# Hybrid state-space block on one core: the head products of two units issued together, their decays and operands a job sooner

## The chip, the cores and the metric

The kernel runs on one core of a Trainium2 chip. The metric is the device time of one execution in microseconds, from the first to the last instruction of that core with what lies around them; less is better. Before the change three runs gave 1990.82, 1993.07 and 1993.24 us (median 1993.07 us).

## The reference, cut to what matters

One layer of a hybrid backbone: a normalised token stream goes through one input projection and is split between a state-space mixer (Mamba-2 style, 32 heads of 64 channels in 4 groups, state 128, chunks of 128 tokens, forward and backward) and a linear recurrent mixer; both are gated, merged, projected, and followed by a gated feed-forward. There are 256 latent and 256 context tokens, model width 2048, all in float32. The change concerns the state-space mixer alone:

```python
CB = jnp.einsum('bcign,bcjgn->bcijg', Cc, Bc)
y_diag = jnp.einsum('bcijg,bcijge,bcjgep->bcigep', CB, Lmat, xdt)
y_off = jnp.einsum('bcign,bcige,bcgepn->bcigep', Cc, jnp.exp(a_cum), entering)
return (y_diag + y_off).reshape(b_, L, G, E, P), final
```

`Lmat` holds the decays between two tokens of a chunk, `exp(a_cum)` those from the start of a chunk. For a latent chunk and a head the output is the sum of three products: the diagonal part (forward and backward decays in one matrix `G`), and the entering states of the two directions times `C` with its decays (`CE`).

## The kernel before, in words

**Projections.** TensorE works through a list of jobs. A job is one 128-column slice of a weight matrix against all 16 tiles of the contraction. `load` brings half a job (a piece, 128x1024 floats, `raw`, line 157) by SP's queue; `parts` splits it into a high part `wh` on ScalarE (line 173) and a low part `wl` on VectorE (line 174). The rings of `raw`, `wh` and `wl` hold four pieces each: the cast of a piece waits until TensorE is done with the piece four before it, and the load of a piece waits until VectorE has made the `wl` four before it. A "both" job (latent and context tokens, lines 188 to 190) and a "lat" job (latent alone, lines 192 to 194) multiply three times per tile of the contraction, a "packed" job (lines 206 and 209) twice. After a job its `evac` empties PSUM, and up to two `rawa` rows of a modulation matrix are multiplied and summed on VectorE (lines 473, loaded at 464); each `rawa` pair stands behind the low parts made so far.

**State-space groups.** For each of four groups of 8 heads there are six "both"/"lat" jobs (four slices of x, one of B, one of C). When the last is done, the group's own work is put into later gaps between jobs, its turns: turn 0 is right behind that job, turn n behind the n-th job after it. Group g's turn 6 is thus group g+1's turn 0; behind the last group come gate jobs ("lat") and then z jobs ("packed"). A turn's parts are issued one behind another on all engines; TensorE's order is the written one, while the order on ScalarE, VectorE and SP is made by a scheduler.

**A group's parts.** `context_tokens`, `context_states` and `carried_states` build transposes, states and the triangular products `U` and `L`. Then there are four units: unit 0 and 1 are chunk 0 and 1 of the first four heads, unit 2 and 3 those of the last four. Each unit has three parts:

- `fetch` (line 802): a DMA copies the unit's cumulated decays to all partitions, tile `AC`, 2 buffers. A third unit's fetch so waits for the first one's products.
- `operands`: ScalarE and VectorE make `E` (lines 811, 812), take two exponentials (line 107), multiply `AC` by `C` (line 817), make `G` from `U` and `L` (820, 821) and multiply it by `E` (line 823). `E` and `G` share 3 buffers.
- `products` (line 840): 24 short float32 matmuls, two heads side by side in the array's columns; VectorE adds the skip term (line 845), and after the second chunk the result goes to memory (line 848).

The turns stand in three tables: `LONG` for groups 0 and 1, `LAST_LONG` for group 2, `SHORT` for group 3. In each row of a table the first entry is for the activations, the second for the three context parts, and the third, fourth and fifth for products, fetch and operands of units 0 to 3.

Of the kernel before, what the change touches and what calls it, by code (L numbers as in the profile page):

```python
# [55 lines left out]
def hybrid_block(  # L56
# [639 lines left out]

    LONG = ((0,), (2, 3, 4), (5, 6, 7, 8), (3, 4, 5, 6), (4, 5, 6, 7))
    LAST_LONG = LONG[:2] + ((5, 6, 8, 10), (3, 4, 5, 7), (4, 5, 6, 8))  # L700
    SHORT = ((0,), (4, 5, 7), (9, 11, 13, 15), (6, 7, 9, 11), (7, 9, 11, 13))

    def xs_evac(g, t):
        def f(ps):
# [6 lines left out]
            if t == 3:  # L711
                when = LONG if g < NG - 2 else LAST_LONG if g < NG - 1 else SHORT
                for ns, fs in zip(when, ssd_group(g)):
# [437 lines left out]
```

## Time and profile before

| | |
|---|---|
| median of three runs | 1993.07 us (1990.82 to 1993.24) |
| the profiled execution: its time, its span | 1992.71 us, 1990.8 us |
| TensorE busy, share of the span | 1961.4 us, 99% |
| VectorE busy | 1425.0 us, 72% |
| ScalarE busy | 1101.9 us, 55% |
| HBM | 220 GB/s over the span |
| the state-space products (line 840) | from 548.1 to 817.1 us |

The busy share of TensorE says that it always had something in flight, not that it was at its peak: ends of matmuls are modelled, and a matmul that starts late or waits for its weights is counted as busy too. What a matmul costs the chain is read from the distance between two starts.

### The profile page before, as it was taken

What the parts mean: (1) busy time and instruction counts of PE and PEld (TensorE: products, weight loads), DVE (VectorE), ACT (ScalarE), POOL (GpSimd) and SP (SyncE); (2) the same over time, 40 slices, a digit from 0 to 9 for tenths busy, and PEclk for the clock granted to TensorE, in tenths of its full rate; (3) what the DMA queues carried; (4) which work ended last, traced back from release to release, by engine and by line L of the source; (5) the groups of instructions that cost most, each with busy time, mean ns of one, the idle gap of its engine ahead of it and who ended that gap; (6) DMA issues with size and microseconds to landing.
All of it is one profiled execution on the core that took longest, in us unless ns stands there. A gap on an engine that the chain in (4) does not pass through costs nothing.

```text
span 1990.8 us, 30569 instructions
## 1 busy us (share of the span) xinstructions
PE 1961.4 (99%) x11649; PEld 1671.6 (84%) x11649; DVE 1425.0 (72%) x2154; ACT 1101.9 (55%) x1663; POOL 3.9 (0%) x7
## 2 busy tenths in 40 slices
PE   7999999999999999999999999999999999999997
PEld 3678888898787798888888888888888888888887
DVE  5468899896767888988787788666666665555553
ACT  4346888784464666755655454544444444444442
POOL 0000000000000000000000000000000000000000
PEclk9999999999999999999999999999999999999999
DMA  9984444456454578899887775777776765566663
GB/s 371 353 289 149 136 155 159 139 187 198 141 163 138 180 223 259 300 322 352 282 288 258 258 266 184 229 235 237 237 233 228 241 219 190 179 188 184 188 192 118
DMA packets 143842, 440.32 MB, mean 221 GB/s; under 512 B 17488, under 2 KB 36176, under 8 KB 143568
## 3 DMA queue, kind: packets, MB, share of 16 engines
q1 hardware_dynamic: 143328, 437.91, 67.0%
q8 instruction: 91, 1.49, 0.3%
q10 hardware_dynamic: 368, 0.47, 0.1%
q14 instruction: 55, 0.45, 0.1%
HBM read 427.77 MB, written 10.55 MB: 220 GB/s over the span
## 4 chain that ended last, share of the span: by engine, by line
PE 58%; issue 38%; DMA 1%; DVE 1%; ACT 1%; POOL 0%; SPq 0%; POOLq 0%; DVEq 0%; ACTq 0%
PE ps L206 14%; PE ps L209 7%; PE ps L188 6%; PE ps L189 5%; PE ps L190 5%; PE ps L192 3%; PE ps L194 3%; PE ps L193 3%; PE ps L391 1%; PE pa L344 1%; PE ps L392 1%; PE ps L393 1%; PE py L840 1%; DMA raw<-in_dram 1%; PE lg L535 1%
## 5 line engine op out<-in xcount | busy, mean ns | idle before, releaser
L174 DVE TENSOR_TENSOR wl<-raw,wh 128x1024 fp32r<-128x1024 f32 (+1 forms) x566 | 677.4, 1199 | 362.9 <-ACT wh L173 359.1
L173 ACT CAST wh<-raw 128x1024 fp32r<-128x1024 f32 (+1 forms) x566 | 580.9, 1030 | 622.9 <-PE ps L206 232.6
L206 PE MATMUL ps<-T,wh 128*128 128x512 f32 x3236 | 822.4, 395 | 0.0
L206 PEld LDWEIGHTS ps<-T,wh 128*128 128x128 f32 x3236 | 577.9, 188 | 111.0 <-issue 0.5
L209 PEld LDWEIGHTS ps<-T,wl 128*128 128x128 f32 x3236 | 439.0, 188 | 37.8
L209 PE MATMUL ps<-T,wl 128*128 128x256 f32 x3236 | 447.8, 280 | 0.0
L188 PE MATMUL ps<-T,wh 128*128 128x512 f32 x464 | 185.6, 400 | 0.0
L190 PE MATMUL ps<-T,wl 128*128 128x512 f32 x464 | 183.2, 395 | 0.0
L189 PE MATMUL ps<-T,wh 128*128 128x512 f32 x464 | 183.2, 395 | 0.0
L473 DVE SCALAR_TENSOR_TENSOR rawa<-rawa,sc 128x1024 f32<-128x1024 f32 x128 | 153.0, 1220 | 30.3 <-DMA rawa<-in_dram 30.1
L192 PE MATMUL ps<-T,wh 128*128 128x256 f32 x576 | 163.2, 283 | 0.0
L194 PE MATMUL ps<-T,wl 128*128 128x256 f32 x576 | 160.9, 279 | 0.0
L193 PE MATMUL ps<-T,wh 128*128 128x256 f32 x576 | 160.8, 279 | 0.0
L192 PEld LDWEIGHTS ps<-T,wh 128*128 128x128 f32 x576 | 108.3, 188 | 2.3 <-issue 1.1
L193 PEld LDWEIGHTS ps<-T,wh 128*128 128x128 f32 x576 | 108.3, 188 | 2.0 <-issue 1.2
L194 PEld LDWEIGHTS ps<-T,wl 128*128 128x128 f32 x576 | 108.2, 188 | 0.0
L188 PEld LDWEIGHTS ps<-T,wh 128*128 128x128 f32 x464 | 87.0, 187 | 22.5 <-issue 1.1
L190 PEld LDWEIGHTS ps<-T,wl 128*128 128x128 f32 x464 | 87.0, 187 | 21.2
L189 PEld LDWEIGHTS ps<-T,wh 128*128 128x128 f32 x464 | 87.0, 188 | 21.1 <-issue 0.7
L107 ACT ACT_TABLE_LOAD x58 | 74.4, 1283 | 1.0
L385 DVE TENSOR_TENSOR wl<-raw,wh 128x896 fp32r<-128x896 f32 x16 | 17.4, 1090 | 46.1 <-ACT wh L384 46.1
L811 ACT ACTIVATE E<-AC,wt 128x128 f32<-128x128 f32 x64 | 20.6, 392 | 49.6 <-DMA AC<-acD 49.6
(246 smaller groups left out, 1866.4 us busy)
## 6 DMA issues: line engine op xcount, KB each, us to landing
raw<-in_dram SPq DMA_DIRECT2D x534, 512.0 KB, 4.6
rawa<-in_dram SPq DMA_DIRECT2D x128, 512.0 KB, 5.8
wa<-in_dram SPq DMA_DIRECT2D x64, 512.0 KB, 7.6
AC<-acD SPq DMA_DIRECT2D x16, 512.0 KB, 6.6
raw<-in_dram SPq DMA_DIRECT2D x16, 448.0 KB, 7.6
raw<-in_dram SPq DMA_DIRECT2D x16, 384.0 KB, 3.3
raw<-in_dram SPq DMA_DIRECT2D x18, 256.0 KB, 2.7
X<-in_dram SPq DMA_DIRECT2D x8, 512.0 KB, 7.2
```

The lines of the kernel that those rows point to most:

```text
L107: i = act.activation(dst, src, func, **kw).ins
L173: act.copy(h[:, :n], raw[:, :n])
L174: held["low"] = dve.tensor_sub(l[:, :n], raw[:, :n], h[:, :n].bitcast(F32)).ins
L188: pe.matmul(ps, wh, T1[:, k, :], start=s, stop=False)
L189: pe.matmul(ps, wh, T2[:, k, :], start=False, stop=False)
L190: pe.matmul(ps, wl, T1[:, k, :], start=False, stop=e)
L192: pe.matmul(ps[:, :T], wh, T1[:, k, :T], start=s, stop=False)
L193: pe.matmul(ps[:, :T], wh, T2[:, k, :T], start=False, stop=False)
L194: pe.matmul(ps[:, :T], wl, T1[:, k, :T], start=False, stop=e)
L206: pe.matmul(ps, wh, job.act(k), start=s, stop=False, skip_group_check=True)
L209: pe.matmul(ps[:, T:], l[:, i % KP, :], job.act(i)[:, :T], start=False, stop=i == last, skip_group_check=True)
L473: i = dve.scalar_tensor_tensor(raw, raw, 1.0, sc[:, h * 1024:h * 1024 + 1024], ALU.mult, ALU.mult, accum_out=MP[:, n, h:h + 1]).ins
```

## The change

Three tables of turns are replaced. In groups 0 and 1 units 0 and 1 multiply at turn 5 and units 2 and 3 at turn 7 (they had a turn each, 5 to 8); in group 2 at turns 5 and 9; in group 3 at turns 11 and 15. Fetches and operands of the first two units come a turn sooner in groups 0 to 2; those of units 2 and 3 come at or right behind the turn of the first pair's products. In group 3 fetches and operands keep their turns.

```diff
-    LONG = ((0,), (2, 3, 4), (5, 6, 7, 8), (3, 4, 5, 6), (4, 5, 6, 7))
-    LAST_LONG = LONG[:2] + ((5, 6, 8, 10), (3, 4, 5, 7), (4, 5, 6, 8))
-    SHORT = ((0,), (4, 5, 7), (9, 11, 13, 15), (6, 7, 9, 11), (7, 9, 11, 13))
+
+    LONG = ((0,), (2, 3, 4), (5, 5, 7, 7), (2, 3, 5, 5), (3, 4, 5, 6))
+    LAST_LONG = LONG[:2] + ((5, 5, 9, 9), (2, 3, 5, 5), (3, 4, 5, 7))
+    SHORT = ((0,), (4, 5, 7), (11, 11, 15, 15), (6, 7, 11, 11), (7, 9, 11, 13))
```

(The fetch row of `SHORT` reads 6, 7, 9, 11 before and 6, 7, 11, 11 now: unit 2's fetch moves with the products that free its buffer.) One line is added above the tables, so from line 700 on a line has a number one higher in the changed kernel.

TensorE at turn 5 of group 0, before; `ps` is a projection, `py` a unit's products:

```order
L188 MATMUL ps<-T_94,wh 128x512
L189 MATMUL ps<-T_95,wh 128x512
L190 MATMUL ps<-T_94,wl 128x512
L840 MATMUL py<-G,xt 64x128 x2
L840 MATMUL py<-AC,s_5120 64x128 x2
L840 MATMUL py<-AC,s_5213 64x128 x2
L840 MATMUL py<-G,xt 64x128 x2
L840 MATMUL py<-AC,s_5120 64x128 x2
L840 MATMUL py<-AC,s_5213 64x128 x2
L188 MATMUL ps<-T_94,wh 128x512
```

And now, what stands between the same two projections:

```order
L841 MATMUL py<-G,xt 64x128 x2
L841 MATMUL py<-AC,s_5122 64x128 x2
L841 MATMUL py<-AC,s_5237 64x128 x2
L841 MATMUL py<-G,xt 64x128 x2
L841 MATMUL py<-AC,s_5122 64x128 x2
L841 MATMUL py<-AC,s_5237 64x128 x2
L841 MATMUL py<-G,xt 64x128 x2
L841 MATMUL py<-AC,s_5234 64x128 x2
L841 MATMUL py<-AC,s_5127 64x128 x2
L841 MATMUL py<-G,xt 64x128 x2
L841 MATMUL py<-AC,s_5234 64x128 x2
L841 MATMUL py<-AC,s_5127 64x128 x2
```

Unit 1's products follow unit 0's with no projection between them. Over the four groups, 16 blocks of products become 8.

VectorE ahead of the last unit's `G` (group 3, unit 3, needed at turn 15), before; `zt` belongs to z jobs, `rawa` to the modulation:

```order
L174 TENSOR_TENSOR wl_7823<-raw_7793,wh_7822 128x1024
L174 TENSOR_TENSOR wl_7857<-raw_7820,wh_7856 128x1024
L306 TENSOR_TENSOR zt_7842<-ps_7803,zt_7842 128x256
L845 SCALAR_TENSOR_TENSOR yt_7864<-XS_6172,V_74,py_7866 128x128
L845 SCALAR_TENSOR_TENSOR yt_7865<-XS_6172,V_74,py_7866 128x128
L917 TENSOR_TENSOR zt_7783<-zt_7783,ldt_7530 128x256
L174 TENSOR_TENSOR wl_7923<-raw_7852,wh_7922 128x1024
L917 TENSOR_TENSOR zt_7842<-zt_7842,ldt_7632 128x256
L817 TENSOR_TENSOR AC_7720<-AC_7720,Cm_6500 128x1024
L823 TENSOR_TENSOR G_7882<-G_7882,E_7881 128x512
L174 TENSOR_TENSOR wl_7957<-raw_7920,wh_7956 128x1024
L473 SCALAR_TENSOR_TENSOR rawa_7860,MP_1272<-rawa_7860,sc_1273 128x1024
```

And the same place now:

```order
L174 TENSOR_TENSOR wl_7906<-raw_7852,wh_7905 128x1024
L822 SCALAR_TENSOR_TENSOR G_7865<-L_7116,wt_1277,G_7865 128x128 x4
L174 TENSOR_TENSOR wl_7940<-raw_7903,wh_7939 128x1024
L473 SCALAR_TENSOR_TENSOR rawa_7860,MP_1272<-rawa_7860,sc_1273 128x1024
L473 SCALAR_TENSOR_TENSOR rawa_7862,MP_1272<-rawa_7862,sc_1273 128x1024
L306 TENSOR_TENSOR zt_7925<-ps_7886,zt_7925 128x256
L918 TENSOR_TENSOR zt_7842<-zt_7842,ldt_7613 128x256
L818 TENSOR_TENSOR AC_7720<-AC_7720,Cm_6524 128x1024
L877 TENSOR_TENSOR sq1_1270<-sq1_1270,sqt_7788 128x256
L824 TENSOR_TENSOR G_7865<-G_7865,E_7864 128x512
```

One more low part and the pair of `rawa` rows 7860 and 7862 now stand ahead of the last `G`, where they stood behind it; the low part of raw_7903 is the one of raw_7920 before.

SP's queue where units 2 and 3 of group 3 are fetched, before (unit 2 is AC_7557, unit 3 AC_7720):

```order
L157 DMA raw_7630<-in_13_dram 128x1024
L802 DMA AC_7557<-acD_101 128x2x512
L157 DMA raw_7659<-in_13_dram 128x1024
L907 DMA ldt_7632<-yD_98 128x256
L157 DMA raw_7691<-in_13_dram 128x1024
L157 DMA raw_7761<-in_13_dram 128x1024
L464 DMA rawa_7699<-in_6_dram 128x1024
L464 DMA rawa_7701<-in_6_dram 128x1024
L802 DMA AC_7720<-acD_101 128x2x512
L157 DMA raw_7793<-in_13_dram 128x1024
```

And now (unit 2 is AC_7718, unit 3 AC_7720):

```order
L157 DMA raw_7672<-in_13_dram 128x1024
L908 DMA ldt_7613<-yD_98 128x256
L157 DMA raw_7761<-in_13_dram 128x1024
L464 DMA rawa_7680<-in_6_dram 128x1024
L464 DMA rawa_7682<-in_6_dram 128x1024
L157 DMA raw_7793<-in_13_dram 128x1024
L803 DMA AC_7718<-acD_101 128x2x512
L157 DMA raw_7820<-in_13_dram 128x1024
L908 DMA ldt_7674<-yD_98 128x256
L803 DMA AC_7720<-acD_101 128x2x512
```

Unit 2's fetch has moved four pieces of weights back in the queue, from behind raw_7630 to behind raw_7793, and unit 3's two places behind it.

## Rows read from the trace of the kernel before

**Rows 1.** The page, part 1: busy us (share of the span) of each engine.
```profile
PE 1961.4 (99%) x11649; PEld 1671.6 (84%) x11649; DVE 1425.0 (72%) x2154; ACT 1101.9 (55%) x1663; POOL 3.9 (0%) x7
```

**Rows 2.** Waits of TensorE over the span: total us, times, longest us.
```profile
PE py L840 <- DVE G L823: 1.2, 1, 1.2
```

**Rows 3.** Timeline of TensorE, unit 0 of group 0: start us, us, instruction.
```profile
547.74 0.39 PE L190 MATMUL ps<-T,wl 128*128 128x512 f32 x1
548.05 0.44 PE L840 MATMUL py<-G,xt 128*64 128x128 f32 x4
...
549.51 0.50 PE L188 MATMUL ps<-T,wh 128*128 128x512 f32 x1
549.86 0.40 PE L189 MATMUL ps<-T,wh 128*128 128x512 f32 x1
550.09 0.39 PE L190 MATMUL ps<-T,wl 128*128 128x512 f32 x1
```

**Rows 4.** Timeline of the weight loads at the same place.
```profile
548.05 0.20 PEld L840 LDWEIGHTS py<-G,xt 128*64 128x64 f32 x4 [0.36 <-issue]
```

**Rows 5.** Timeline of TensorE, context products alone (group 0).
```profile
511.94 0.40 PE L190 MATMUL ps<-T,wl 128*128 128x512 f32 x1
...
514.17 0.39 PE L189 MATMUL ps<-T,wh 128*128 128x512 f32 x1
```

**Rows 6.** Timeline of TensorE, unit 3 of group 0 joined to group 1's context products.
```profile
586.28 0.39 PE L190 MATMUL ps<-T,wl 128*128 128x512 f32 x1
...
590.11 0.39 PE L189 MATMUL ps<-T,wh 128*128 128x512 f32 x1
```

**Rows 7.** Timeline of TensorE, the last unit (group 3, unit 3).
```profile
815.81 0.44 PE L840 MATMUL py<-G,xt 128*64 128x128 f32 x4 [1.23 <-DVE G L823]
```

**Rows 8.** Busy us by engine ahead of it: stretch, PE, PEld, DVE, ACT, POOL, PEclk, DMA.
```profile
795.00:816.00 21.00, 19.77 (x133) 17.07 (x133) 18.30 (x36) 17.56 (x31) 0.00 (x0) 1.00 0.88 285
```

**Rows 9.** Timeline of VectorE, the same stretch.
```profile
801.02 1.23 DVE L812 SCALAR_TENSOR_TENSOR E<-AC,wt,E 128x128 f32<-128x128 f32 x4 [1.12 <-ACT E L811]
802.83 1.22 DVE L174 TENSOR_TENSOR wl<-raw,wh 128x1024 fp32r<-128x1024 f32 x1 [0.58 <-ACT wh L173]
803.98 1.22 DVE L473 SCALAR_TENSOR_TENSOR rawa<-rawa,sc 128x1024 f32<-128x1024 f32 x1
...
807.00 0.42 DVE L306 TENSOR_TENSOR zt<-ps,zt 128x256 f32<-128x256 f32 x1
807.33 1.14 DVE L821 SCALAR_TENSOR_TENSOR G<-L,wt,G 128x128 f32<-128x128 f32 x4
...
813.93 1.22 DVE L817 TENSOR_TENSOR AC<-AC,Cm 128x1024 f32<-128x1024 f32 x1 [0.54 <-ACT AC L107]
815.07 0.68 DVE L823 TENSOR_TENSOR G<-G,E 128x512 f32<-128x512 f32 x1
```

**Rows 10.** Timeline of SP's queue at unit 3's fetch.
```profile
791.90 0.39 SPq L802 DMA_DIRECT2D AC<-acD  x1
792.95 1.47 SPq L157 DMA_DIRECT2D raw<-in_dram  x2
```

**Rows 11.** Timeline of ScalarE, where it waits for that fetch.
```profile
800.59 0.69 ACT L811 ACTIVATE E<-AC,wt 128x128 f32<-128x128 f32 x2 [2.05 <-DMA AC<-acD]
```

**Rows 12.** All 16 fetches (line 802), from issue to landing.
```profile
DMA to landing us min/median/max: 4.8/6.6/9.5
```

**Rows 13.** Busy us by engine and granted clock, behind the mixer's end (columns as in rows 8).
```profile
1232.04:1238.87 6.83, 5.07 (x15) 4.32 (x16) 6.83 (x19) 4.82 (x11) 0.00 (x0) 0.50 0.02 9
```

**Rows 14.** Timeline of TensorE at the same place.
```profile
1233.80 2.90 PE L228 MATMUL ps<-T,wh 128*128 128x512 f32 x6 [2.23 <-DVE T L1051]
...
1237.78 2.06 PE L228 MATMUL ps<-T,wh 128*128 128x512 f32 x6
...
1240.39 1.56 PE L228 MATMUL ps<-T,wh 128*128 128x512 f32 x6
...
1242.50 1.56 PE L228 MATMUL ps<-T,wh 128*128 128x512 f32 x6
```

## The prediction

> **What bounds the kernel now.** The page's first part says TensorE: busy for 99% of the span, VectorE for 72% [rows 1]. The list of TensorE's waits shows one in the state-space groups: 1.2 us for the last unit's `G` [rows 2]. So a change here acts in two ways: in what the written order costs TensorE, and in whether the operands are there. For the first I read its timeline at one unit. Projections follow each other by 0.23 us (549.86 to 550.09), and the 24 products stand between the starts 547.74 and 549.86 [rows 3]. These 2.12 us hold two projection steps (0.47), so a lone unit costs 1.65 us. Inside, the products go in 12 pairs; from 548.05 to 549.51 is 1.46 us, the last 0.20 of them the way back to a projection. A pair is about 0.11, 12 of them 1.31, so 0.34 us of a lone unit is getting in and out: the first weight load comes 0.36 us after the one before it has ended [rows 4].
>
> For the second I read the stretch ahead of the last unit. VectorE is busy 18.3 of 21 us and ScalarE 17.6 [rows 8], while TensorE waits 1.23 us before 815.81 [rows 7]. What stands on VectorE ahead of the last `G` sets the end there, and what a fetch holds up on ScalarE.
>
> **The change, part by part.** *Joined products.* Before, 13 units stand alone, 13 x 1.65 = 21.5 us. Three stand right before the next group's context products: such a block takes 586.28 to 590.11, 3.83 us [rows 6], against 2.23 for context products alone [rows 5], so a unit there adds 1.60; 4.8 for three. Now 8 blocks have two units each: 1.65 + 1.31 = 2.96, 23.7 in all. Saved: 21.5 + 4.8 - 23.7 = 2.6 us. The bounds for a joint: nothing saved, or the whole 0.34; I take the whole, since pairs inside a unit go on without a break when the head changes. Of the 2.6, 1.9 are saved before turn 11 of group 3.
>
> By the Trainium skill's page "TensorE: Matmul & The Clock Gate", section "Part 2: What happens when you issue a matmul", TensorE pulls a weight load ahead of matmuls in flight, so getting in would cost nothing. Rows 4 say that it doesn't do so between these two kinds. By the rule nothing would be saved, which is the last rival below.
>
> *Decays and operands sooner, groups 0 to 2.* The same instructions and the same 16 fetches move by a turn; none is added. Where unit 2's and 3's fetches come with the first pair's products they have two turns until they are needed. ScalarE and VectorE do them beside the projections; the cover is the ring of four pieces. In these groups TensorE waits for no `G` today [rows 2], so there is nothing to win. I take 0; the upper bound is the only such wait in the trace, 1.2 us. POOL's queue isn't touched.
>
> *Group 3, turns 11 to 15.* This is where I expect the gain to be given back.
> - When TensorE is ready. Before, it stood ready for unit 3 at 815.81 - 1.23 = 814.6. Now it is 1.9 sooner by the earlier joints; of group 3, three lone units (4.95) have become one pair (2.96), 2.0 sooner: it reaches the pair of turn 15 at 810.7. Unit 2 takes 0.1 + 1.3, so unit 3's operands are wanted at 812.1.
> - When unit 2's fetch lands. Its buffer is free once unit 0 has multiplied, now at turn 11 instead of 9. On SP it stands behind raw_7793, whose load was issued at 792.95 [rows 10]. That load waits for a low part on VectorE, which comes 1.9 sooner with TensorE and some 2.2 sooner because unit 2's two groups of four short operations (lines 812 and 821, 1.1 to 1.2 each [rows 9]) no longer stand ahead of it: 788.9, and the fetch at 789.2. With the median of 6.6 us [rows 12] it lands at 795.8; with the ends 4.8 and 9.5, at 794.0 or 798.7. Below about 795 VectorE is still busy with other work.
> - What VectorE has to do from there to the last `G`, in the new order: two groups on line 812 (1.2 each), two on line 821 (1.1), five low parts (1.15), four `rawa` rows (1.15), three sums on line 306 and two products on line 917 (0.33), two each on lines 817 (1.14) and 823 (0.65), one of 0.33 on line 876 (as line 306) [rows 9]: 2.4 + 2.2 + 5.75 + 4.6 + 1.65 + 2.3 + 1.3 + 0.3 = 20.5 us. A low part waits 0.6 for its cast, as at 802.83. The two `rawa` rows and the low part that now stand ahead of the last `G` are 3.4 of this. Nothing lies beside them: VectorE is one queue.
> - So the last `G` is done at 795.8 + 0.4 (the first of ScalarE's four) + 21.1 = 817.3, and TensorE waits 5.2 us instead of 1.2. It starts the last unit at 817.3 instead of 815.8: 1.5 us later than before, for all the joints. Ends: 795 + 0.4 + 20.5 = 815.9 without the wait for a cast, level with before, and 798.7 + 21.5 = 820.2, 4.4 late. Behind it nothing is late: the `rawa` pair is done, the ring full.
>
> *TensorE's clock.* So long a wait has its price. At the end of the mixer TensorE waited three times, last for 2.23 us before 1233.80, and its granted clock was 0.50, the 1.2 GHz level, from 1232.04 to 1238.87, 1.00 after it [rows 13, 14]. The first projection steps of the next stage then took 1233.80 to 1237.78 and 1237.78 to 1240.39, 3.98 and 2.61 us, against 2.11 (1240.39 to 1242.50): 2.4 us lost [rows 14]. The single wait of 1.23 before 815.81 cost no clock (1.00 in rows 8). Between 0 and 2.4 I take 1.5: 5 us is nearer to the place where it fell, but part of the slow stretch may lie in the wait. The same page, section "Why this matters for your kernels", warns of idle gaps between bursts of matmuls, and the fall in rows 13 agrees. Taken strictly it gives the whole 2.4 and 1996.6.
>
> *Sum.* +1.5 + 1.5 = +3.0 us on the profiled execution's 1992.71 us, which stands 0.36 under the median of the three runs: **1995.7 us**, +0.15%. A measurement of this kernel tells about 0.2%, 4.0 us, from no change, so this counts as the same. This case's own range is 1992.7 (nothing later, no clock lost) to 1996.7.
>
> **The rivals.**
> - *The last `G` comes in time.* If VectorE and ScalarE run the new order tighter than I add it up (a fetch that lands in 4.8 us, no cast in the way), the wait stays at 1.2 or goes. Then the joints' 2.6 are the gain, 1990.1, or 3.8 with the wait gone, 1988.9. For it: VectorE's 2.7 idle us in rows 8. Against it: 3.4 us more stand ahead of that `G`, and TensorE wants it 2.5 sooner. Chance 0.15; a third of it, next to the bound, may be measured beyond 0.2%.
> - *Slower: the fetch lands late.* In this very stretch unit 3's fetch took from 791.90 to 800.59, 8.7 us [rows 10, 11], and ScalarE stood still for it, with casts queued behind. Two fetches now share the queue with weights. At 789.2 + 8.7 = 797.9 the last unit starts at 819.4, 3.6 late, and with 1.5 of clock that is 5.1: 1997.8. It decides from a landing at 796.8 on, 7.6 us after the issue: there the whole is over 4.0. Chance 0.22.
> - *The joints save nothing* (another bank in PSUM and other weights cost as much as a projection between). Rows 5 and 6 speak for it, where a joint with context products saved 0.05; the even pairs inside a unit against it. TensorE and all that follows it come 1.9 later, the last unit at 819.2, 3.4 late; with 1.5 of clock 1997.6. Chance 0.05. The skill's rule on weight loads, named above, comes to the same time.
>
> **How the numbers follow.** The forecast has 0.58. Faster by over 0.2%: a third of the first rival, 0.05. Slower by over 0.2%: 0.22 + 0.05 = 0.27. Within: 0.58 + 0.10 = 0.68. The range goes from the joints' full gain, 1990.0, to the late fetch with some more clock lost, 1998.5; it leaves out the first rival's far part and the worst landings.
>
> **What would show it.** In the changed profile: 8 blocks of 48 products, each 2.96 us of TensorE's path; no wait for `G` before 800 us; unit 2's fetch of group 3 issued near 789 and landing near 796; VectorE full from there, with the `rawa` pair ahead of the last `G`; a wait of TensorE on line 841 of about 5 us ending near 817; a stretch of granted clock 0.50 right after it. I am wrong if that wait is under 2 us, if a joint costs more than 0.1, or if TensorE waits in groups 0 to 2 for operands or casts.

## The result, and the profile after

The changed kernel takes 2003.8 us (median of five runs, 2002.89 to 2006.68) against 1992.85 us for the kernel before in the same comparison: a ratio of 1.0063 (95% interval 1.0051 to 1.0074), 11 us slower by the medians and 12.5 by the ratio. A second comparison gave 2001.55 us and 1.0052 (1.0039 to 1.0064). Forecast were 1995.7 us and a range up to 1998.5; the result lies outside it.

Page of the changed kernel, part 1 (answers to [rows 1]):

```profile
PE 1965.1 (98%) x11649; PEld 1674.5 (84%) x11649; DVE 1424.7 (71%) x2154; ACT 1099.6 (55%) x1663; POOL 3.9 (0%) x7
```

No engine has more instructions or, apart from TensorE, more work. The time went into waits. Those of TensorE, changed kernel (line, what it waited for; total us, times, longest; the other lines of the list name places where the kernel before waits too):

```profile
PE py L841 <- DVE G L824: 5.6, 2, 5.0
PE p L773 <- DVE xw L737: 3.6, 1, 3.6
...
PE ps L206 <- ACT wh L173: 0.7, 1, 0.7
```

The longest of the first line, 5.0 us, was forecast (5.2). The second line, in group 3's `context_states`, was not. How much each place costs can be read from one projection's start in two traces. The one that starts at 833.25 us before, behind the last unit (254.51 is a projection ahead of the state-space groups),

```profile
254.51 0.28 PE L192 MATMUL ps<-T,wh 128*128 128x256 f32 x1
...
833.25 0.63 PE L209 MATMUL ps<-T,wl 128*128 128x256 f32 x4
```

starts in the changed kernel at 848.09:

```profile
257.03 0.28 PE L192 MATMUL ps<-T,wh 128*128 128x256 f32 x1
...
848.09 0.63 PE L209 MATMUL ps<-T,wl 128*128 128x256 f32 x4
```

That is 14.8 us later. 2.5 of them were there before the first state-space operation (257.03 against 254.51) and belong to this execution, not to the change: in the second profiled execution of the changed kernel they are -0.1. A fall of the granted clock goes with them: near 28 us it is 0.50 in this execution. It falls there in seven of the fourteen profiled executions, long before any turn of a table; these seven reach that first projection 1.5 to 2.7 us later than the kernel before, the others within 0.5 us of it. So the groups cost 12.3 us more in the one and 9.8 in the other. Below, "cost of the groups" is always this difference between the same two projections, taken in the profiled execution.

**The joints** came out as forecast. TensorE, changed kernel, units 0 and 1 of group 0 (answers to [rows 3]):

```profile
550.24 0.39 PE L190 MATMUL ps<-T,wl 128*128 128x512 f32 x1
550.55 0.44 PE L841 MATMUL py<-G,xt 128*64 128x128 f32 x4
...
553.33 0.50 PE L188 MATMUL ps<-T,wh 128*128 128x512 f32 x1
553.66 0.40 PE L189 MATMUL ps<-T,wh 128*128 128x512 f32 x1
```

From 550.24 to 553.66 are 3.42 us, with two projection steps (0.47) in them: 2.95 for two units, forecast 2.96. Up to 701 us the offset to the kernel before had fallen by 1.2 us; no wait stands in groups 0 and 1. In group 2 there is a short one, for the second unit of the pair at turn 9 (the second wait in the first line of the list above):

```profile
734.21 0.44 PE L841 MATMUL py<-G,xt 128*64 128x128 f32 x4 [0.55 <-DVE G L824]
```

**The place that the forecast missed.** TensorE at group 3's `context_states`, before:

```profile
747.23 0.28 PE L194 MATMUL ps<-T,wl 128*128 128x256 f32 x1
747.35 1.04 PE L743 MATMUL px<-K,XS 128*128 128x128 f32 x8
...
751.25 0.68 PE L192 MATMUL ps<-T,wh 128*128 128x256 f32 x1
```

and now:

```profile
748.68 0.28 PE L194 MATMUL ps<-T,wl 128*128 128x256 f32 x1
748.79 1.15 PE L744 MATMUL px<-K,XS 128*128 128x128 f32 x8
753.51 2.07 PE L773 MATMUL p<-xw,Bt 128*128 128x512 f32 x2 [3.57 <-DVE xw L737]
755.38 1.91 PE L774 MATMUL p<-xw,Bt 128*128 128x512 f32 x2
757.08 1.85 PE L773 MATMUL p<-xw,Bt 128*128 128x512 f32 x2
758.77 1.02 PE L774 MATMUL p<-xw,Bt 128*128 128x512 f32 x2
759.23 0.68 PE L192 MATMUL ps<-T,wh 128*128 128x256 f32 x1
```

From projection to projection it is 10.55 us instead of 4.02: 3.57 of wait, and another 2.96 because the matmuls behind it run at half the clock (pairs 1.7 to 1.9 us apart, 0.86 before). Counted from the start of the matmul that waited to the next projection, the clock's share is 2.7 us (5.72 against 3.03); the listed wait is some 0.3 short. The chain behind it starts on SP, with the fetches of group 3's units 0 and 1, changed kernel:

```profile
737.69 0.38 SPq L803 DMA_DIRECT2D AC<-acD  x1
...
738.74 0.67 SPq L803 DMA_DIRECT2D AC<-acD  x1
```

Before, the first was issued at 727.75, when group 2's unit 2 had multiplied (turn 8) and its `AC` buffer was free. Now both buffers are held until group 2's pair at turn 9. ScalarE, changed kernel, stands at `E` for the landing:

```profile
745.32 0.99 ACT L812 ACTIVATE E<-AC,wt 128x128 f32<-128x128 f32 x3 [9.13 <-DMA AC<-acD]
```

(before: 2.54 us, until 734.55). Two casts and the copy of `Bt` stand behind it. VectorE, changed kernel, stands too, and then does what the scheduler had put ahead of `xw`:

```profile
745.75 0.94 DVE L813 SCALAR_TENSOR_TENSOR E<-AC,wt,E 128x128 f32<-128x128 f32 x3 [4.86 <-ACT E L812]
747.28 1.23 DVE L174 TENSOR_TENSOR wl<-raw,wh 128x1024 fp32r<-128x1024 f32 x1 [0.59 <-ACT wh L173]
...
749.35 1.22 DVE L174 TENSOR_TENSOR wl<-raw,wh 128x1024 fp32r<-128x1024 f32 x1
750.48 1.22 DVE L473 SCALAR_TENSOR_TENSOR rawa<-rawa,sc 128x1024 f32<-128x1024 f32 x1
...
751.63 1.22 DVE L473 SCALAR_TENSOR_TENSOR rawa<-rawa,sc 128x1024 f32<-128x1024 f32 x1
...
752.77 2.48 DVE L737 TENSOR_TENSOR xw<-px,wt 128x512 f32<-128x512 f32 x4
```

`xw` starts at 752.77; before it started at 745.65, ahead of `context_states`. The Trainium skill's page "Perfetto Trace Analysis", section "Tensor Engine Instruction (MATMUL, LD_WEIGHTS)", calls ScalarE's and VectorE's queues strict first-in-first-out; the 9.13 and 4.86 us of standing with ready work behind agree.

**The last unit**, TensorE, changed kernel (answers to [rows 7]):

```profile
821.38 0.44 PE L841 MATMUL py<-G,xt 128*64 128x128 f32 x4
...
827.95 0.69 PE L841 MATMUL py<-G,xt 128*64 128x128 f32 x4 [5.04 <-DVE G L824]
...
830.71 3.54 PE L206 MATMUL ps<-T,wh 128*128 128x512 f32 x8
```

The granted clock, changed kernel (us from:to, length, busy us of PE, PEld, DVE, ACT, POOL; clock, DMA; answers to [rows 13]):

```profile
751.92:758.75 6.83, 5.24 (x6) 2.13 (x7) 6.83 (x16) 4.82 (x10) 0.00 (x0) 0.50 0.90 356
827.01:833.84 6.83, 5.89 (x31) 4.92 (x32) 6.83 (x16) 4.50 (x9) 0.00 (x0) 0.50 0.82 282
```

Each wait has a stretch at 0.50, the 1.2 GHz level, that begins before the wait ends and lasts 5.2 to 5.9 us beyond it; the profiled execution of the kernel before had none between its start and 1232 us. The last pair with its step takes 9.54 us (821.17 to 830.71); without a wait such a pair takes 2.98. So 5.04 is wait, 1.52 the slower products, and the projections up to 833.8 lose another 1.4, since they come 0.43 apart instead of 0.23: 2.9 for the clock, or 2.7 counted from the start of the matmul that waited.

### The profile page after: what moved, and what is told of

Read it like the earlier page. It is cut to its first block, busy times and chain, and to the rows that moved or that the text cites. A ratio compares the mean times of both kernels' runs of the same rounds, so it can differ in the third digit from the quotient of the medians.

```text
span 2003.9 us, 30561 instructions
## 1 busy us (share of the span) xinstructions
PE 1965.1 (98%) x11649; PEld 1674.5 (84%) x11649; DVE 1424.7 (71%) x2154; ACT 1099.6 (55%) x1663; POOL 3.9 (0%) x7
## 3 DMA queue, kind: packets, MB, share of 16 engines
HBM read 427.77 MB, written 10.55 MB: 219 GB/s over the span
## 4 chain that ended last, share of the span: by engine, by line
PE 57%; issue 38%; DMA 2%; DVE 2%; ACT 1%; POOL 0%; POOLq 0%; SPq 0%; DVEq 0%; ACTq 0%
PE ps L206 14%; PE ps L209 7%; PE ps L188 5%; PE ps L189 5%; PE ps L190 5%; PE ps L194 3%; PE ps L193 3%; PE ps L192 3%; PE ps L391 1%; PE ps L392 1%; PE ps L393 1%; PE pa L344 1%; PE py L841 1%; DMA wa<-in_dram 1%; DMA AC<-acD 1%
## 5 line engine op out<-in xcount | busy, mean ns | idle before, releaser
L206 PE MATMUL ps<-T,wh 128*128 128x512 f32 x3236 | 823.3, 396 | 0.7 <-ACT wh L173 0.7
L188 PE MATMUL ps<-T,wh 128*128 128x512 f32 x464 | 185.4, 400 | 0.0
L189 PE MATMUL ps<-T,wh 128*128 128x512 f32 x464 | 183.2, 395 | 0.0
L391 PE MATMUL ps<-T,wh 128*128 128x512 f32 x112 | 47.5, 424 | 0.0
```

The source lines that it names most:

```text
L188: pe.matmul(ps, wh, T1[:, k, :], start=s, stop=False)
L189: pe.matmul(ps, wh, T2[:, k, :], start=False, stop=False)
L206: pe.matmul(ps, wh, job.act(k), start=s, stop=False, skip_group_check=True)
```

## Experiments

All runs compute the reference in full; only the turns differ. "Groups" is the cost of the groups as defined above, in us against the kernel before; turns are those of units 0 to 3.

| run | products in groups 0, 1 / 2 / 3 | median us | ratio (95%) | groups |
|---|---|---|---|---|
| changed kernel | 5,5,7,7 / 5,5,9,9 / 11,11,15,15 | 2003.8 | 1.0063 (1.0051 to 1.0074) | +12.3 |
| the same again | same | 2001.55 | 1.0052 (1.0039 to 1.0064) | +9.8 |
| sooner, not joined | 5,6,7,8 / 5,6,8,10 / 9,11,13,15 | 1992.07 | 0.9996 (0.9987 to 1.0005) | -0.8 |
| groups 0, 1 only | 5,5,7,7 / 5,6,8,10 / 9,11,13,15 | 1991.35 | 0.9997 (0.9988 to 1.0006) | -0.7 |
| groups 0 to 2 only | 5,5,7,7 / 5,5,9,9 / 9,11,13,15 | 1996.19 | 1.0015 (1.0006 to 1.0024) | +2.5 |
| group 3 only | 5,6,7,8 / 5,6,8,10 / 11,11,15,15 | 1998.59 | 1.0033 (1.0021 to 1.0046) | +7.8 |
| group 2's pair at 8 | 5,5,7,7 / 5,5,8,8 / 11,11,15,15 | 2005.3 | 1.0069 (1.0055 to 1.0083) | +12.6 |
| last pair at 17 | 5,5,7,7 / 5,5,9,9 / 11,11,17,17 | 1996.29 | 1.0021 (1.0012 to 1.0030) | +3.3 |
| group 2's last two apart | 5,5,7,7 / 5,5,8,10 / 9,11,13,15 | 1990.52 | 0.9988 (0.9979 to 0.9997) | -2.1 |
| both cures | 5,5,7,7 / 5,5,8,10 / 11,11,17,17 | 1992.66 | 0.9999 (0.9991 to 1.0008) | -0.1 |
| pairs at 9 and 17 | 5,5,7,7 / 5,5,8,10 / 9,9,17,17 | 1988.8 | 0.9981 (0.9972 to 0.9990) | -3.6 |
| group 2's pair at 10 | 5,5,7,7 / 5,5,10,10 / 11,11,17,17 | 1994.48 | 1.0011 (1.0002 to 1.0020) | +2.0 |
| at 10, then 9 and 17 | 5,5,7,7 / 5,5,10,10 / 9,9,17,17 | 1992.92 | 1.0003 (0.9995 to 1.0012) | +1.2 |

The kernel before had medians of 1992.05 to 1992.85 us beside these. The median's distance from its own and the cost of the groups agree within 1.4 us (2.0 for group 3 only), so the timed differences lie in the groups.

### Which part costs?

My theory: two places, each with its own cause; the joints are sound. First the second half of the change alone, fetches and operands sooner and nothing joined (against the kernel before):

```diff
-    LONG = ((0,), (2, 3, 4), (5, 6, 7, 8), (3, 4, 5, 6), (4, 5, 6, 7))
-    LAST_LONG = LONG[:2] + ((5, 6, 8, 10), (3, 4, 5, 7), (4, 5, 6, 8))
+    LONG = ((0,), (2, 3, 4), (5, 6, 7, 8), (2, 3, 5, 6), (3, 4, 5, 6))
+    LAST_LONG = LONG[:2] + ((5, 6, 8, 10), (2, 3, 5, 6), (3, 4, 5, 7))
```

> The kernel before with the other half of the change alone: in groups 0 to 2 fetches and operands a job sooner (fetches at turns 2, 3, 5, 6, operands at 3, 4, 5, 6 or 7), all products where they were, nothing joined. Theory: these groups had slack, and group 3's buffers come free as before; no wait of TensorE goes or comes, 0 +- 1 us: about 1992.3 us. Rival: the sooner operands load ScalarE and VectorE at the wrong turns (low parts and casts late, or xw of a context part); then TensorE waits 1 us or more in groups 0 to 2 and the time is 1994 us or more.

Measured 0.9996; no new wait. The sooner operands cost and bring nothing that can be told.

Then the change in groups 0 and 1 alone (the new `LONG`, the old `LAST_LONG` and `SHORT`):

```diff
-    LONG = ((0,), (2, 3, 4), (5, 6, 7, 8), (3, 4, 5, 6), (4, 5, 6, 7))
+    LONG = ((0,), (2, 3, 4), (5, 5, 7, 7), (2, 3, 5, 5), (3, 4, 5, 6))
```

> Only groups 0 and 1 have the new tables; groups 2 and 3 keep the old ones. Theory: the joints save what the forecast says, and nothing in these groups waits. Two groups had 3 lone units (1.65 us each) and one unit next to context products (1.60), 6.55 us a group; now 2 blocks of 2.96, 5.92. So 2 x 0.63 = 1.3 us sooner, about 1991.6 us, no new wait of TensorE, granted clock 1.00 through the groups, and the last unit waits for its G as before (about 1 to 2.5 us, since TensorE comes 1.3 sooner). Rival: part of the loss stems from groups 0 and 1 (an order of ScalarE or VectorE that costs TensorE without a listed wait): then the kernel is 1 us or more slower than before.

The ratio, 0.9997, cannot tell 1.3 us; the trace can. A projection behind group 0 and 1 stands 0.27 us late at 701 us where it was 1.50 late before the groups: 1.2 us saved. The last `G` is then waited for 1.7 us instead of 1.2, which takes part of it back.

With group 2's new table as well (against the run before this one):

```diff
-    LAST_LONG = LONG[:2] + ((5, 6, 8, 10), (3, 4, 5, 7), (4, 5, 6, 8))
+    LAST_LONG = LONG[:2] + ((5, 5, 9, 9), (2, 3, 5, 5), (3, 4, 5, 7))
```

> Groups 0 to 2 have the new tables, group 3 the old one. Theory: group 2's second pair, now at its turn 9, frees both AC buffers late; group 3's first two fetches land late, ScalarE stands about 9 us at E of group 3's unit 0 and VectorE makes xw late. So context_states of group 3 waits about 3.6 us for xw (line 737) and the granted clock falls to 0.50 behind it: +6.5 us, less 1.9 us for the joints of three groups: about 1997.5 us. Rival: the late xw comes from group 3's own new turns; then there is no wait there and the kernel comes 1 to 2 us sooner than before, about 1991.

TensorE at `context_states` of this run:

```profile
752.67 2.07 PE L773 MATMUL p<-xw,Bt 128*128 128x512 f32 x2 [3.16 <-DVE xw L737]
```

Group 3's table is the old one here, and the run before, without group 2's table, has no such wait, so it is group 2's table that makes `xw` late: the offset jumps by 5.1 us (1.13 to 6.20). 1.1 of it come back at the last unit, whose `G` is now all but in time (0.2 us).

And group 3's new table alone, against the kernel before:

```diff
-    SHORT = ((0,), (4, 5, 7), (9, 11, 13, 15), (6, 7, 9, 11), (7, 9, 11, 13))
+    SHORT = ((0,), (4, 5, 7), (11, 11, 15, 15), (6, 7, 11, 11), (7, 9, 11, 13))
```

> Only group 3 has the new table. Theory: the two bad places are independent. No wait at group 3's context_states; the last unit's G is late as in the changed kernel: TensorE waits 5 us there (line 841), the granted clock falls to 0.50 behind it, and by the offsets of the changed kernel the whole place costs 6.9 us net of its joints: about 1999.7 us. Rival: the last wait is a consequence of the earlier disturbance (fetches and weights pushed back at 740 to 760 us); then the wait is 1 to 2.5 us, the clock stays at 1.00, and the time is within 2 us of the kernel before.

Waits of TensorE in this run:

```profile
PE ps L206 <- ACT wh L173: 2.8, 1, 2.8
PE py L841 <- DVE G L824: 2.2, 1, 2.2
```

The sum is 5.0 us as expected, but it is split: unit 2's fetch (issued 792.28) holds ScalarE for 4.74 us until 801.54, unit 3's for another 1.04, and the cast of a piece behind them comes late. Only then is `G` waited for, 2.2 us. The clock falls behind each. So the place has two faults: the casts behind ScalarE's wait, and VectorE's full queue ahead of `G`. That casts are queued there the prediction said only in a rival, without a price.

The changed kernel once more, to see whether the first profile was typical:

> The changed kernel itself once more, with more rounds. If the two bad places cause the loss, every profile has both waits (3 to 4 us for xw at line 773 near 750 us, 5 us for the last G at line 841 near 822 us) with the granted clock at 0.50 behind each, and the ratio stays near 1.006 (about 2004 us). If the first profile was an unlucky one, one of the waits is missing or under 2 us.

It was, with smaller sizes:

```profile
PE py L841 <- DVE G L824: 5.3, 2, 5.0
...
PE p L773 <- DVE xw L737: 2.8, 1, 2.8
```

The shorter wait for `xw` and its clock cost 4.8 us here instead of 6.5 (8.82 us from projection to projection).

### What makes `xw` late?

Group 2's pair a turn sooner frees the buffers sooner (against the changed kernel, as all that follow where nothing else is said):

```diff
-    LAST_LONG = LONG[:2] + ((5, 5, 9, 9), (2, 3, 5, 5), (3, 4, 5, 7))
+    LAST_LONG = LONG[:2] + ((5, 5, 8, 8), (2, 3, 5, 5), (3, 4, 5, 7))
```

> The changed kernel, but group 2's second pair multiplies at turn 8 instead of 9, so both AC buffers come free a turn (some 10 us) sooner; all else is as in the changed kernel. Theory: group 3's first fetches are issued by about 728 and land by about 737, ScalarE doesn't stand at E, and the wait of 3.6 us for xw goes with the stretch of 0.50 behind it: 6.5 us less than the changed kernel, about 1997.3 us; the wait of 5 us for the last G stays. Rival: xw is late because the scheduler put other work (a pair of rawa rows and a low part) ahead of it on VectorE, whatever the fetches do; then the wait stays at 2 us or more and the time within 3 us of the changed kernel's 2003.8.

TensorE of this run at group 2's second pair:

```profile
723.66 0.44 PE L841 MATMUL py<-G,xt 128*64 128x128 f32 x4
...
730.74 0.70 PE L841 MATMUL py<-G,xt 128*64 128x128 f32 x4 [5.55 <-DVE G L824]
```

The wait for `xw` is gone, as the theory has it, though TensorE itself stands 5.2 us late by then, so that this run alone doesn't show that `xw` is in time; the next one does. The wait for the last `G` stays (5.0 us). Yet no time is won (expected 1997.3, measured 2005.3): unit 3, which stood at turn 10 before, is now wanted at turn 8, and its exponentials come on ScalarE only at 727.77, behind the activation of `XS` and a table load. The clock falls there instead. A pair moves the need for its second unit forward as well as the release of its first unit's buffer back.

So the pair is undone in group 2, with the early operands kept, and group 3 as before:

```diff
-    LAST_LONG = LONG[:2] + ((5, 5, 9, 9), (2, 3, 5, 5), (3, 4, 5, 7))
-    SHORT = ((0,), (4, 5, 7), (11, 11, 15, 15), (6, 7, 11, 11), (7, 9, 11, 13))
+    LAST_LONG = LONG[:2] + ((5, 5, 8, 10), (2, 3, 5, 5), (3, 4, 5, 7))
+    SHORT = ((0,), (4, 5, 7), (9, 11, 13, 15), (6, 7, 9, 11), (7, 9, 11, 13))
```

> Groups 0 and 1 as changed; in group 2 units 0 and 1 as changed (one block at turn 5), but units 2 and 3 apart again at turns 8 and 10 as in the kernel before; group 3 as before. Theory: with one AC buffer free at turn 8, group 3's first fetch lands before ScalarE wants it, no wait for xw, no 0.50 there, no wait for G in group 2 (as there was when the pair stood at turn 8). Joints: 1.26 + 0.34 = 1.6 us saved; the last unit's G is waited for 1 to 2.5 us as before. About 1991.2 us. Rival: fetches and operands a turn sooner in group 2 are what disturbs ScalarE and VectorE there; then TensorE waits 2 us or more for xw or for a G, and the time is 1995 us or more.

1990.52 us. The fetch is issued at 728.21 and `E` starts at 734.94; no wait for `xw`, and the last `G` costs 0.7 us.

Does the late buffer alone do it? With the pair at turn 10 the buffers come free later still, but the scheduler there puts `xw` ahead of `E` on VectorE (against the run "last pair at 17"):

```diff
-    LAST_LONG = LONG[:2] + ((5, 5, 9, 9), (2, 3, 5, 5), (3, 4, 5, 7))
+    LAST_LONG = LONG[:2] + ((5, 5, 10, 10), (2, 3, 5, 5), (3, 4, 5, 7))
```

> The run with the last pair at turn 17, but group 2's second pair a turn later still, at its turn 10 (next to group 3's context products): both AC buffers come free even later, but VectorE's order now has the four xw ahead of group 3's first four operations on E (in the changed kernel E, a low part and a rawa pair stand ahead of xw). Theory: what makes xw late is not the late buffer as such but that VectorE and ScalarE stand at E, ahead of xw, while the fetch is under way; so the wait for xw in context_states goes though the fetch lands later (issued about 741, landed about 748 to 754). The jump of 5.1 us at that place in the last-pair-at-17 run goes: 1996.3 - 5.1 = about 1991 us. Rival: the late buffers hold the group up in any case, through ScalarE, where casts and copies of the context parts stand behind E: a wait of 2 us or more on a cast, on s0 or on xw between 745 and 765 us, and 1995 us or more.

ScalarE of this run,

```profile
747.06 1.28 ACT L812 ACTIVATE E<-AC,wt 128x128 f32<-128x128 f32 x4 [8.26 <-DMA AC<-acD]
```

its TensorE,

```profile
744.84 0.28 PE L194 MATMUL ps<-T,wl 128*128 128x256 f32 x1
744.96 1.04 PE L744 MATMUL px<-K,XS 128*128 128x128 f32 x8
...
748.87 0.68 PE L192 MATMUL ps<-T,wh 128*128 128x256 f32 x1
```

and its waits:

```profile
PE ps L206 <- ACT wh L173: 3.4, 2, 2.2
...
PE ps L209 <- DVE wl L174: 0.6, 2, 0.4
PE ps L194 <- DVE wl L174: 0.5, 1, 0.5
```

ScalarE stands 8.26 us, nearly as long as in the changed kernel, and `context_states` takes 4.03 us, as before the change. So it is not the late landing as such; it is the late landing together with an order in which `xw` stands behind `E` in VectorE's queue. The 5.1 us at that place went as expected. The time did not follow (1994.48 instead of 1991), because TensorE, now earlier, meets the casts that are late behind group 3's two fetches (3.4 us). In the run with the last pair at 17, where TensorE stood 3 to 5 us late, that wait was 0.9 us; that its own delay hid the rest is the reading, not a separate test.

### The last unit

Two turns more for the last pair, everything else as changed; VectorE's order ahead of the last `G` stays the same:

```diff
-    SHORT = ((0,), (4, 5, 7), (11, 11, 15, 15), (6, 7, 11, 11), (7, 9, 11, 13))
+    SHORT = ((0,), (4, 5, 7), (11, 11, 17, 17), (6, 7, 11, 11), (7, 9, 11, 13))
```

> The changed kernel, but the last pair of group 3 multiplies at turn 17 instead of 15; its fetches and operands keep their turns, and VectorE's order ahead of the last G stays word for word. Theory: that G is done near 828 us as in the changed kernel, TensorE now reaches it two turns (about 12.9 us) later, so the wait of 5.0 us and the stretch of 0.50 behind it (2.7 us) go; the wait for xw in group 3's context_states (3.6 us and its clock) stays. 2003.8 - 7.7 = about 1996.1 us. Rival: what hurts there is ScalarE standing for the two fetches with casts queued behind it; then TensorE waits for a cast (line 206) instead, 2 us or more, the clock falls all the same, and the time is 1999 us or more.

1996.29 us, as the theory has it. Waits of TensorE in this run:

```profile
PE p L773 <- DVE xw L737: 2.9, 1, 2.9
...
PE ps L206 <- ACT wh L173: 0.9, 1, 0.9
```

The `G` wait and the second stretch at 0.50 are gone; `xw` and a cast remain.

### Both cures, and a version that beats both kernels

```diff
-    LAST_LONG = LONG[:2] + ((5, 5, 9, 9), (2, 3, 5, 5), (3, 4, 5, 7))
-    SHORT = ((0,), (4, 5, 7), (11, 11, 15, 15), (6, 7, 11, 11), (7, 9, 11, 13))
+    LAST_LONG = LONG[:2] + ((5, 5, 8, 10), (2, 3, 5, 5), (3, 4, 5, 7))
+    SHORT = ((0,), (4, 5, 7), (11, 11, 17, 17), (6, 7, 11, 11), (7, 9, 11, 13))
```

> Both cures: group 2's last two units apart at turns 8 and 10, group 3's last pair at turn 17; all other blocks joined as in the change. Theory: no wait for xw, none for G, granted clock 1.00 through the state-space groups; joints save 1.26 in groups 0 and 1, 0.34 in group 2, 0.68 in group 3, and the old wait of 1.2 us for the last G is gone: 3.5 us sooner than the kernel before, about 1989.3 us. Rival: ScalarE's two fetches in a row (turn 11) hold casts up, TensorE waits 1 to 3 us on line 206 and the clock falls there: then 1991 to 1995 us.

Waits of TensorE in this run:

```profile
PE ps L206 <- ACT wh L173: 1.2, 1, 1.2
...
PE ps L209 <- DVE wl L174: 0.5, 2, 0.3
```

1992.66 us: the rival was right about the place and the time, though the clock stayed at 1.00. Both long waits are gone, and the casts behind the two fetches of turn 11 eat what was won. `context_states` also took 5.01 us instead of 4.02: `xw` starts at 746.92 here, 1.3 us later than before, with TensorE 1.1 us earlier, and two weight loads wait 0.35 and 0.90 us for it (747.65 and 748.85), which a list of the waits of matmuls leaves out.

The remedy is to let those fetches go before the z jobs' own work grows, with the first pair at turn 9 (against both cures; the operands of units 1 to 3 come two turns sooner as well):

```diff
-    SHORT = ((0,), (4, 5, 7), (11, 11, 17, 17), (6, 7, 11, 11), (7, 9, 11, 13))
+    SHORT = ((0,), (4, 5, 7), (9, 9, 17, 17), (6, 7, 9, 9), (7, 7, 9, 11))
```

> As the run with both cures, but group 3's first pair multiplies at turn 9 instead of 11, with the fetches of units 2 and 3 at turn 9 too; the last pair stays at turn 17. Theory: the same joints; AC buffers come free two turns sooner, so the last G has some 8 turns of slack, and casts have more room before the z jobs' own work: no waits, about 1989.3 us, within 1 us of the run with both cures. Rival: the first pair at turn 9 needs unit 1's operands (wanted two turns sooner) before they are there: a wait on line 841 near 782 us of 2 us or more and a clock fall: 1993 us or more.

1988.8 us, ratio 0.9981 (0.9972 to 0.9990): faster than the kernel before by 3 to 4 us (2.0 to 5.6 by the interval). TensorE waits nowhere in the groups, and the projection at 833.25 before starts at

```profile
829.76 0.63 PE L209 MATMUL ps<-T,wl 128*128 128x256 f32 x4
```

in this run: 3.5 us earlier. Seven of the eight joints are in it, and the old wait of 1.2 us [rows 2] is gone.

Finally the eighth joint back, group 2's pair at 10 (against the run just told):

```diff
-    LAST_LONG = LONG[:2] + ((5, 5, 8, 10), (2, 3, 5, 5), (3, 4, 5, 7))
+    LAST_LONG = LONG[:2] + ((5, 5, 10, 10), (2, 3, 5, 5), (3, 4, 5, 7))
```

> All eight blocks joined as in the change, with other turns: group 2's second pair at 10, group 3's pairs at 9 and 17. Theory: all the joints (2.6 us) and one more next to context products (about 0.1), the old wait of 1.2 us gone, no wait for xw; unit 0's and 1's operands of group 3 have from the landing of their fetches (748 to 754) until turn 9 (about 773). About 3.8 us sooner than the kernel before, 1988.3 us, level with the run of pairs at 9 and 17 with group 2's last units apart (1988.8). Rival: the fetches of group 3's first units land so late that its first pair is waited for at turn 9 (line 841, 2 us or more, clock 0.50 behind it): 1992 us or more.

A miss: 1992.92 us, level with the kernel before. ScalarE in this run:

```profile
750.96 1.28 ACT L812 ACTIVATE E<-AC,wt 128x128 f32<-128x128 f32 x4 [9.93 <-DMA AC<-acD]
```

And TensorE's waits:

```profile
PE ps L194 <- DVE wl L174: 2.0, 2, 1.0
...
PE ps L209 <- DVE wl L174: 0.5, 1, 0.5
```

Neither `xw` nor a `G` is waited for, as in the theory; but ScalarE's standing makes casts late, behind them low parts, and TensorE pays for these in pieces of 0.2 to 1.0 us.

## Why the prediction was wrong

- **Joined products, -2.6.** Right. 2.95 us a pair against 2.96; the changes in groups 0 and 1 alone saved 1.2 of 1.3. The rival by which joints save nothing has fallen. The pulling ahead of weight loads that the Trainium skill's page "TensorE: Matmul & The Clock Gate", section "Part 2: What happens when you issue a matmul", states doesn't show at this switch between kinds of matmuls: in the changed kernel too, the first weight load of a pair starts 0.36 us after the one before it has ended.
- **Decays and operands sooner, groups 0 to 2: 0, at most 1.2.** This is the step that failed. For the operands themselves it holds (0.9996 alone). But it asked only what could be won, from waits that were in the trace, and let the pair of group 2 cost nothing. That pair holds both `AC` buffers until turn 9, where one came free at turn 8 before; group 3's first fetch goes out 10 us later, and ScalarE and VectorE stand at `E` with `xw` behind: 6.5 us in the first profile, 4.8 in the second, 5.1 with group 3 as before. The pair also made TensorE wait in its own group, 0.55 us for `G` at 734.21, which was one of the prediction's signs of being wrong.
- **Group 3, turns 11 to 15.** The mechanism was right: a wait of 5.04 us for 5.2 forecast. From ScalarE's first `E` (806.06) to the end of `G` (827.9) are 21.8 us; forecast were 21.5. Not counted was a cast that is late behind ScalarE's wait, 0.7 us in the changed kernel and 2.8 with group 3's table alone. Unit 2's fetch was issued at 798.54. Ahead of group 3's turns TensorE stood 8.0 us behind the kernel before, where the forecast had it 1.9 ahead; less these 9.9 us the issue is at 788.7 (forecast 789.2) and, 7.4 us later (6.6), the landing at 796.1 (795.8), short of the 796.8 from which the rival of the late fetch was to decide. With group 3's table alone, where TensorE stood 1.7 us behind, the same count gives an issue at 788.7 and, 9.2 us later, a landing at 797.9: there that rival came true.
- **TensorE's clock, 1.5 once (0 to 2.4).** Mis-sized and counted once: it fell twice, for 2.96 and 2.9 us (2.7 each, counted from the start of the matmul that waited). I took less than the 2.4 of [rows 14] because part of a slow stretch may lie in the wait. Little does: behind the wait came 5.07 us of it there (1233.80 to 1238.87), 5.24 and 5.89 here.
- **Sum.** 3.0 forecast, plus 6.5 for the missed place, 1.4 for the clock and 0.7 for the cast, is 11.6 of the 12.3 us in the groups of that execution. The wait of 0.55 in group 2 makes it 12.2.

The range failed for the same reason as the sum: no case in it let a wait arise ahead of turn 11 of group 3. The prediction's last sentence comes near it (waits in groups 0 to 2 for operands or casts), but no chance stood against that.

## What to carry to other kernels

When steps are put together, ask of each buffer that they hold when it now comes free, who fetches into it next (here the next group), and what stands behind that fetch on the in-order engines: in this kernel a release 10 us later cost 4.8 to 6.5 us, while the joint that it bought was worth 0.3. Joining also moves the need for the second step forward; give it the turn of the later one, or leave it alone where the release matters. And a wait that a cure removes may have hidden the next one: in two runs the cure of one place was given back at the casts behind another.

## What was unexpected in the hardware

The long waits in the groups were dearer than their length: the granted clock fell to 0.50 with waits of 2.8, 2.9, 3.16, 3.57, 5.04 and 5.55 us in these runs, and with the changed kernel's two it cost 2.7 us on top each time. With 1.7 us in one run, 1.8 in another, and 2.2 with 1.2 ahead of it in a third, it stayed at 1.00; yet with 2.2 us at the last unit of the run with group 3's table alone, shortly after an earlier slow stretch, it fell. Near 28 us, where TensorE has waited on and off from the start, it fell in seven of the fourteen profiled executions, the longest wait just before being 1.3 to 2.3 us; in the other seven, with waits of 1.25 to 1.83 us, it did not. What decides between these was not tried. The fetch of 128x1024 cumulated decays, 4.8 to 9.5 us before [rows 12], took up to 12.4 in the changed kernel, where two go out within 1.1 us of each other.
